# A rank for each kind of operation in attention's build-time order, and each head pair's gate projected in the pair's first two steps

## The chip, the core and the metric

The kernel runs on one core of a Trainium2 chip. The metric is the time on the device of one execution, in microseconds (us); lower is better. Seven streams of instructions matter here. PE is TensorE (matrix products and transposes; PEld is its weight load), DVE is VectorE, ACT is ScalarE, POOL is GpSimd, and SP issues the DMAs. Each engine runs its own queue strictly in order, and an instruction that waits for another engine holds up all that stands behind it in its queue.

## What is computed

A decoder trunk of two layers over 1024 tokens of width 1024: a Mamba-2 layer, then a stick-breaking attention layer, each with a residual add and a gated per-layer embedding (PLE) behind it. The change lies in the attention layer alone:

```python
def stick_breaking_mixer(h, k, v, norm_g, w_in, q_g, w_out):
    qg = rmsnorm(h, norm_g) @ w_in
    gate = qg[..., SB_WIDTH:]
    q = rmsnorm(qg[..., :SB_WIDTH].reshape(bsz, s, SB_HEADS, SB_HEAD_DIM), q_g)
    ...
    for blk in range(s // SB_BLOCK):
        z = jnp.einsum('bhtd,bhsd->bhts', q[:, :, q0:kend], k[:, :, :kend])
        ...
        log_keep = jnp.where(strict, jax.nn.log_sigmoid(-z), 0.0)
        suffix = lax.cumsum(log_keep, axis=3, reverse=True) - log_keep
        weights = jnp.where(strict, jnp.exp(jax.nn.log_sigmoid(z) + suffix), 0.0)
        outs.append(jnp.einsum('bhts,bhsd->bhtd', weights, v[:, :, :kend]))
    return (o * jax.nn.silu(gate)) @ w_out
```

There are 16 heads of 64, so 8 pairs of heads. Queries, keys, values and gate are projected from the normalized residual stream; the products are made in three terms (high times high, high times low, low times high half of each operand) for accuracy.

## The kernel before

**Stages.** The trace has the Mamba layer and its PLE first, then attention from about 926 us, then the second PLE with the rest of the output projection (`layer_b2`) from about 1646 us to the end.

**Attention's work.** The loop runs over 8 head pairs `hp`, and in each over four steps `p` = 3, 2, 1, 0, a step being two blocks of 128 tokens. Tokens are reversed, so step 3 sees the fewest keys and step 0 the most. The index `i` counts the 32 steps. One step consists of these operations, each of them one entry of a plan:

- `project` (L905): per block 24 products of 384 columns into a PSUM tile `mm` (keys, values, queries), cut into chunks of two. `copy_kq` and `copy_v` (L944, L946) take it out on ACT.
- `gate` (L905, 512 columns, 24 products a half): the pair's gate, in two halves. `sig` (L971, ACT) and `gmul` (L973, DVE) turn a half into `GT`.
- `norm`: `square` (L1010, ACT), `sums` (L1016), `start` (L1022 to L1024), three Newton turns `newton` (L1028 to L1030) and `nmul` (L1037), all on DVE.
- `values`: SP shifts V by one row (`vs`, L982 to L987), POOL subtracts and splits it (L991 to L1001).
- `flip` (L1048, PE): transposes the step's keys and queries; `k_hi` and `q_hi` (L1058, L1070, ACT) and `k_lo` and `q_lo` (L1061, L1075, DVE) split them.
- `scores` (L1104, L1105, PE): products `z` of 128 to 512 columns; `s_sig` (L1112, ACT) makes sigmoids `pt`; `scan` (L1117, DVE) runs the stick-breaking product along the row. Steps 1 and 0 have two parts a block (320 and 384, 448 and 512 columns), steps 3 and 2 one (128 and 256, 384 and 512).
- `combine`: `turn` (L1142, L1144, PE) transposes weights into `tr`; `a_hi` (L1150, ACT) and `a_lo` (L1155, DVE) split them into `wh` and `wl`; `prod` (L1163, PE) multiplies with V into `oq`; `o_copy` (L1178), `o_add` (L1183) and `o_gate` (L1190) finish the rows.
- `weights`: the next pair's weights, four loads `raw` of 512 KB (L1219), split by `w_hi` (L1238, ACT) and `w_lo` (L1242, DVE) in 16 pieces each. The `raw` tiles come from a ring of three.
- At the end `s_out` loads and splits the output weights (L1256, L1266, L1273) and `fill` multiplies two token blocks with them (48 products each, L1314; its sums are added by L1326). Behind the plan stand the PLE weights (loads L674, split L174 and L178), which take the same `raw` ring.

**What sets the order.** `Plan.order` works at build time. Of all operations whose predecessors are placed and whose ring slots are free it takes the one that could start first by its own estimates of durations; among those that could start at the same time the lowest `rank` goes first, then the one that was written first. The outcome is the order in which PE, ACT and DVE get their instructions. Ranks are 10·i plus a small number by kind: `combine` 10·i, `norm` 10·i+1, `flip` 10·i+2, `scores` 10·i+3, `project` and `gate` 10·i+5. All projections and gates are chained one behind the other in the order in which they are written (`mm_last`); in `before` the gate's two halves stand between the two blocks of step 1.

Of the kernel before, what the change touches and what calls it, by code (L numbers as in the profile page):

```python
# [18 lines left out]
P = 128  # L19
# [23 lines left out]


# [19 lines left out]
class Plan:  # L64
# [789 lines left out]
def attention(k, A, rawp, hT, oTd, dbg, b2, pairs):  # L854


    tc, nc = k.tc, k.nc
# [3 lines left out]
    with ExitStack() as ctx:  # L861
# [22 lines left out]
        op_, slot = plan.op, plan.slot  # L884
# [11 lines left out]
        def chunks(rank, us, m, make, prs, after_of, first=()):  # L896

            rec, ids = slot("mm"), []
            for c in range(0, len(prs), m):
                def go(c=c):  # L900
                    if c == 0:
                        make()
                    for i in range(c, min(c + m, len(prs))):
                        a, b, out = prs[i]()
                        nc.tensor.matmul(out, lhsT=a, rhs=b, start=(i == 0), stop=(i == len(prs) - 1))  # L905
                after = list(after_of(c, min(c + m, len(prs)) - 1))
                after += ids[-1:] if c else list(first) + mm_last[-1:]
# [9 lines left out]
        def project(i, hp, b):  # L917
            p = b // 2
            key = ("ps", hp, b)

            def make():
                tiles[key] = mm.tile([P, 512], F32, name="mm")
            sl = slice(b % 4 * P, b % 4 * P + P)
            prs = []
            for kk in range(KT):
                for t in range(3):
                    def pr(kk=kk, t=t):
                        w = sts[hp]["W"][kk]
# [3 lines left out]
            rec, ids = chunks(10 * i + 5, 0.175, 2, make, prs, wdeps(hp))  # L932
# [12 lines left out]
            a = op_("ACT", 0.37, 10 * i + 1, copy_kq, ids[-1:], takes)  # L945
            v = op_("ACT", 0.27, 10 * i + 1, lambda: nc.scalar.copy(sts[hp]["vr"][p][:, b % 2], tiles[key][:, 128:256]),  # L946
                    [a], (), (rec,))
            return a, v

        def gate(i, hp, half):  # L950
# [12 lines left out]
            rec, ids = chunks(10 * i + 5, 0.232, 2, make, prs, wdeps(hp))  # L963
# [8 lines left out]
            a = op_("ACT", 0.6, 10 * i + 2, sig, ids[-1:])  # L972
            gmul[hp, half] = op_("DVE", 0.69, 10 * i + 2, lambda: nc.vector.tensor_tensor(  # L973
                sts[hp]["GT"][:, sl], tiles[key], sts[hp]["GT"][:, sl], op=ALU.mult), [a], (), (rec,))

        def values(i, hp, p, copies):
# [12 lines left out]
            vd[i] = op_("SPV", 3.0, 10 * i, load, list(copies) + ([fgate[i - 4]] if i >= 4 else []), (vs_s,),  # L989
                        (vr_s[i - 1],) if p < 3 else ())  # L990
            sub = op_("POOL", 0.74, 10 * i, lambda: nc.gpsimd.tensor_tensor(  # L991
# [10 lines left out]
            vready[hp, p] = op_("POOL", 1.8, 10 * i, split, [sub], (V_s[i],), (vs_s,))  # L1002

        def norm(i, hp, p, copies):
# [6 lines left out]
            sq = op_("ACT", 0.63, 10 * i + 1, square, copies, (sg_s,))  # L1011
# [5 lines left out]
            rd = op_("DVE", 0.68, 10 * i + 1, sums, [sq], (), (sg_s,))  # L1017
# [20 lines left out]
            nmul[i] = op_("DVE", 0.69, 10 * i + 1, mul, [x])  # L1038

        def flip(i, hp, p):  # L1040
# [11 lines left out]
            fk = op_("PE", 0.22, 10 * i + 2, turn_(0), [nmul[i]], (ks,))  # L1052
            fq = op_("PE", 0.22, 10 * i + 2, turn_(1), [fk], (qs,), (kq_s[i],))
# [23 lines left out]
            for h in range(2):  # L1077
                prev = [op_("ACT", 0.47, 10 * i + 2, key_hi(h), [fk] + prev + (old if p == 3 else []))]
                khi[i, h] = prev[0]
                pd = [op_("DVE", 0.49, 10 * i + 2, key_lo(h), [khi[i, h]] + pd, (), (ks,))]  # L1080
                klo[i, h] = pd[0]
            for h in range(2):
                prev = [op_("ACT", 0.73, 10 * i + 2, query_hi(h), [fq] + prev, (qh_s,) if h == 0 else ())]
                pd = [op_("DVE", 0.43, 10 * i + 2, query_lo(h), prev + pd + old, (), (qs,))]
                qlo[i, h] = pd[0]
# [6 lines left out]
        def scores(i, hp, h, b, qh_s):  # L1092
# [4 lines left out]
            last = []  # L1097
            for m, (ko, w) in enumerate(parts(b)):
# [7 lines left out]
                z = op_("PE", 2 * (0.013 + w * 0.000419), 10 * i + 3, mul, [klo[i, h], qlo[i, h]] + last[:1], (z_s,), (qh_s,))  # L1106
# [6 lines left out]
                s = op_("ACT", 0.19 + w * 0.00078, 10 * i + 3, sig, [z], (pt_s[i, h, b],) if m == 0 else (), (z_s,))  # L1113
# [5 lines left out]
                last = [z, op_("DVE", 0.15 + w * 0.00208, 10 * i + 3, scan, [s] + last[1:])]  # L1119
            scans[i, h, b] = last[1]  # L1120

        def combine(i, hp, p):
            lo = 2 * p
            of_s = slot("of")
            for h in range(2):
                pr = None
                for j0 in range(lo, NT, 2):
# [17 lines left out]
                    T = op_("PE", 0.109 * c / P, 10 * i, turn_, [scans[i, h, lo], scans[i, h, lo + 1]], (tr_s,),  # L1145
# [5 lines left out]
                    H = op_("ACT", 0.2 + c * 0.00076, 10 * i, high, [T], (w_s,))  # L1151
# [4 lines left out]
                    L = op_("DVE", 0.16 + c * 0.00103, 10 * i, low, [H], (), (tr_s,))  # L1156
# [16 lines left out]
                    pr = op_("PE", 2 * c * 0.00047, 10 * i, mul, after, (), gives)  # L1173
# [5 lines left out]
                c_ = op_("ACT", 0.37, 10 * i, copy, [pr], (of_s,) if h == 0 else ())  # L1179
# [4 lines left out]
                fadd[i, h] = op_("DVE", 0.42, 10 * i, add, [c_])  # L1184
# [7 lines left out]
            fgate[i] = op_("DVE", 0.8, 10 * i, gates, [fadd[i, 0], fadd[i, 1], gmul[hp, p // 2], vd[i]], (), (of_s,))  # L1192
            if hp == 7:
                x = [fgate[i], begun[0]]
                for b in (2 * p + 1, 2 * p):
                    sl = slice(b * P, (b + 1) * P)
                    a = op_("ACT", 0.31, 10 * i, lambda b=b, sl=sl: nc.scalar.copy(b2.rows(b)[0], sts[7]["GT"][:, sl]), x)
                    rows_done[b] = op_("DVE", 0.28, 10 * i, lambda b=b, sl=sl: nc.vector.tensor_tensor(
                        b2.rows(b)[1], sts[7]["GT"][:, sl], b2.rows(b)[0].bitcast(F32), op=ALU.subtract), [a])
            elif p == 0:  # L1200
                def store():
                    nc.sync.dma_start(oTd[hp * P:(hp + 1) * P, :], sts[hp]["GT"])
                    if "oT" in dbg:
                        nc.sync.dma_start(dbg["oT"][hp * P:(hp + 1) * P, :], sts[hp]["GT"])
                stored.append(op_("SPS", 3.0, 10 * i, store, [fgate[i]]))
# [4 lines left out]
        def weights(hp, q):  # L1210

            rank = 40 * hp - 12 + 2 * q
# [7 lines left out]
            ld = op_("SPW", 3.5, rank, load, [proj[hp - 1, 7 - 2 * q][0]], (r_s,))  # L1220
            small = (4 * hp + q) % 6 == 3
            pool, bufs, seq = (pairs.more, 2, ring2) if small else (pairs.pool, 10, ring10)
            for j in range(2):
# [4 lines left out]
                for m in range(2):  # L1228
# [14 lines left out]
                    dep = [op_("ACT", 0.5, rank, high, [ld] + old + dep)]  # L1243
                    done.append(op_("DVE", 0.5, rank, low, dep, (), (r_s,)))
                wready[hp, kk] = done

        def s_out(kk):
# [9 lines left out]
            ld = op_("SPW", 3.5, rank, load, [proj[7, 5][0]], (r_s,))  # L1257
# [10 lines left out]
            a = op_("ACT", 1.06, rank, high, [ld] + old + list(first)[:1])  # L1268
# [5 lines left out]
            sdone[kk] = (a, op_(eng, us, rank, low, [a], (), (r_s,)))  # L1274
# [3 lines left out]
        def fill(t, rank, extra, takes, places):  # L1278
# [9 lines left out]
            ld = op_("SPW", 4.0, rank - 20, load, extra + stored, (r_s,) + takes)  # L1288
# [11 lines left out]
            a = op_("ACT", 1.3, rank - 20, split(0), [ld])  # L1300
            l = op_("POOL", 2.4, rank - 20, split(1), [a], (), (r_s,))
            recs = [slot("mm"), slot("mm")]
            ids = []
            for q in range(2):
                for m in range(2):
                    for c in range(0, 12, 6):
# [13 lines left out]
                        ids.append(op_("PE", 1.38, rank, go, after, takes_))  # L1320
            mm_last.append(ids[-1])
            for m in range(2):
# [5 lines left out]
                op_("DVE", 0.69, rank, add, [ids[-1]], (), (recs[m],))  # L1328
            return ids[-1]

        for hp in range(8):
            pair = [(4 * hp + 3 - p, p) for p in (3, 2, 1, 0)]
            for i, p in pair:
                copies = project(i, hp, 2 * p + 1)
                if p == 1:
                    gate(i, hp, 1)
                    gate(i, hp, 0)
# [6 lines left out]
            if hp == 6:  # L1344
                begun.append(op_("SPW", 0.0, 0, lambda: b2.begin(pairs), proj[6, 0][-1:]))
# [255 lines left out]
```

## Time and profile before

| | us |
|---|---|
| median of 3 runs (1839.4 to 1842.2) | 1841.28 |
| the profiled execution | 1838.35 |
| its span in the trace | 1836.6 |
| attention, start to the last product of `fill` | 926 to about 1646 |
| one head pair in the middle of it | about 83.5 |
| PE busy, share of the span | 95% |
| DVE busy, share of the span | 65% |

The shares are means over the whole span. In attention DVE's load is higher than its mean, and PE's lower. A time in the trace counts from the start of the span.

### The profile page before, as it was taken

The numbers are of one execution on the slowest core, as the hardware profiler recorded it, in microseconds if no ns is written. First come the engines' busy times: TensorE is split into PE (matmuls) and PEld (weight loads), VectorE is DVE, ScalarE is ACT, GpSimd is POOL, SyncE is SP. The second block draws the span as 40 slices with busy tenths as digits, with TensorE's granted clock in tenths as the row PEclk, the third lists the DMA queues.
The fourth block names the chain that finished last, engine by engine and source line by source line (L and its number), as shares of the span: only waits on it lengthen the run. The fifth ranks groups of instructions, "written<-read, shape, count | busy, mean of one in ns | idle before, by whom it ended". The sixth has DMA issues, their size and how long they took to land.

```text
span 1836.6 us, 25614 instructions
## 1 busy us (share of the span) xinstructions
PE 1740.1 (95%) x9170; PEld 1465.8 (80%) x9170; DVE 1198.9 (65%) x2460; ACT 904.5 (49%) x1976; POOL 416.6 (23%) x452
## 2 busy tenths in 40 slices
PE   7999999999999999999998989898989989789999
PEld 6777877877876877888887879898888878678887
DVE  6687278279169554345567787879787877782332
ACT  6567358349337332124456465656555555561221
POOL 0234534524625122200011110111111012220110
PEclk9999999999999999999999999999999999899999
DMA  4223213223212754322211111111111112151110
GB/s 155 66 81 92 81 62 94 92 60 96 92 52 87 245 158 149 116 97 76 95 41 29 53 29 41 31 43 30 53 43 31 44 38 64 61 175 62 50 38 35
DMA packets 96399, 139.43 MB, mean 76 GB/s; under 512 B 18160, under 2 KB 66640, under 8 KB 96272
## 3 DMA queue, kind: packets, MB, share of 16 engines
q1 hardware_dynamic: 96272, 137.80, 23.4%
q8 instruction: 72, 1.18, 0.3%
q14 instruction: 55, 0.45, 0.1%
HBM read 108.77 MB, written 24.77 MB: 73 GB/s over the span
## 4 chain that ended last, share of the span: by engine, by line
PE 78%; DVE 14%; ACT 5%; issue 2%; DMA 2%; POOL 0%; SPq 0%; DVEq 0%; ACTq 0%
PE mm L48 37%; PE mm L905 18%; PE mm L1432 4%; DVE pt L1117 3%; PE oq L1163 3%; PE pq L48 2%; PE z L1105 2%; DVE v L304 2%; PE intra L479 2%; DVE wl L1155 2%; PE z L1104 2%; PE tr L1142 1%; PE inter L474 1%; PE tr L734 1%; PE tr L1144 1%
## 5 line engine op out<-in xcount | busy, mean ns | idle before, releaser
L48 PE MATMUL mm<-ul,wh 128*128 128x512 f32 (+1 forms) x648 | 254.0, 392 | 0.0
L48 PE MATMUL mm<-uh,wl 128*128 128x512 f32 (+1 forms) x648 | 252.4, 390 | 0.0
L48 PE MATMUL mm<-uh,wh 128*128 128x512 f32 (+1 forms) x648 | 252.4, 389 | 0.1
L1117 DVE TENSOR_TENSOR_SCAN pt<-pt,keep 128x320 f32<-128x320 f32 (+3 forms) x192 | 190.8, 1021 | 7.9 <-ACT pt L1112 2.5
L905 PE MATMUL mm<-g0h,hh 128*128 128x384 f32 x512 | 177.1, 346 | 0.0
L905 PE MATMUL mm<-g0l,hh 128*128 128x384 f32 x512 | 176.1, 344 | 0.7 <-DVE g0l L1242 0.7
L905 PE MATMUL mm<-g0h,hl 128*128 128x384 f32 x512 | 176.2, 344 | 0.0
L304 DVE SCALAR_TENSOR_TENSOR v<-u,convh,v 128x512 f32<-128x512 f32 x144 | 129.5, 904 | 55.1 <-ACT v L302 52.6
L991 POOL TENSOR_TENSOR vs<-vs,vr 128x256 f32<-128x256 f32 x32 | 23.9, 747 | 559.7 <-DMA vs<-vr 182.7
L48 PEld LDWEIGHTS mm<-ul,wh 128*128 128x128 f32 x648 | 121.7, 188 | 26.1 <-issue 2.3
L48 PEld LDWEIGHTS mm<-uh,wh 128*128 128x128 f32 x648 | 121.7, 188 | 25.7 <-issue 1.1
L48 PEld LDWEIGHTS mm<-uh,wl 128*128 128x128 f32 x648 | 121.8, 188 | 25.6 <-issue 1.9
L176 POOL TENSOR_TENSOR wl<-raw,wh 128x1024 fp32r<-128x1024 f32 x39 | 95.3, 2443 | 156.0 <-ACT wh L174 156.0
L1150 ACT CAST wh<-tr 128x512 fp32r<-128x512 f32 (+1 forms) x160 | 82.5, 548 | 71.3 <-PE tr L1144 71.1
L1155 DVE TENSOR_TENSOR wl<-tr,wh 128x512 fp32r<-128x512 f32 (+1 forms) x160 | 96.6, 632 | 22.9 <-ACT wh L1150 21.7
L1112 ACT ACTIVATE pt<-z 128x320 f32<-128x320 f32 (+3 forms) x192 | 88.7, 490 | 45.8 <-PE z L1105 45.2
L644 DVE SCALAR_TENSOR_TENSOR acc<-mm,rg,acc 128x512 f32<-128x512 f32 x64 | 47.9, 749 | 84.5 <-PE mm L48 83.4
L905 PEld LDWEIGHTS mm<-g0l,hh 128*128 128x128 f32 x512 | 98.0, 191 | 1.8 <-DVE g0l L1242 1.1
L905 PEld LDWEIGHTS mm<-g0h,hh 128*128 128x128 f32 x512 | 98.1, 192 | 1.1
L905 PEld LDWEIGHTS mm<-g0h,hl 128*128 128x128 f32 x512 | 97.7, 191 | 0.5
L717 DVE SCALAR_TENSOR_TENSOR pth<-pth,pq 128x512 f32<-128x512 f32 (+1 forms) x33 | 22.2, 672 | 114.5 <-PE pq L48 109.7
L1104 PE MATMUL z<-kst,qh 128*128 128x320 f32 (+3 forms) x192 | 75.4, 394 | 13.4 <-ACT qh L1070 5.7
(378 smaller groups left out, 4347.6 us busy)
## 6 DMA issues: line engine op xcount, KB each, us to landing
raw<-in_w_in SPq DMA_DIRECT2D x40, 512.0 KB
ex<-acd SPq DMA_DIRECT2D x64, 256.0 KB
raw<-in_w_b SPq DMA_DIRECT2D x32, 512.0 KB
raw<-in_m_out SPq DMA_DIRECT2D x16, 512.0 KB
raw<-in_gate SPq DMA_DIRECT2D x16, 512.0 KB
graw<-gT SPq DMA_DIRECT2D x30, 256.0 KB
gT<-zs SPq DMA_DIRECT2D x28, 256.0 KB
acc<-in_x SPq DMA_DIRECT2D x8, 512.0 KB
```

Of the source, the lines that this page charges most:

```text
L48: nc.tensor.matmul(out, lhsT=a, rhs=b, start=(i == 0), stop=(i == n - 1))
L176: (eng or nc.gpsimd).tensor_tensor(lo, raw, hi.bitcast(F32), op=ALU.subtract)
L304: nc.vector.scalar_tensor_tensor(vv, u[:, 3 - j:3 - j + 512], w(j), vv, op0=ALU.mult, op1=ALU.add)
L644: nc.vector.scalar_tensor_tensor(acc[:, sl], ps, k.rg[:, g, t:t + 1], acc[:, sl], op0=ALU.mult, op1=ALU.add)
L905: nc.tensor.matmul(out, lhsT=a, rhs=b, start=(i == 0), stop=(i == len(prs) - 1))
L1104: nc.tensor.matmul(z[:, :w], lhsT=tiles["qh", i][:, h, qs], rhs=rk, start=True, stop=False)
L1112: nc.scalar.activation(tiles[key][:, ko:ko + w], tiles["z", i, h, b, m][:, :w], AF.Sigmoid, scale=-1.0)
L1117: nc.vector.tensor_tensor_scan(pt[:, ko:ko + w], pt[:, ko:ko + w], keep[:, ko:ko + w], pt[:, ko - 1:ko] if ko else 1.0, op0=ALU.mult, op1= ...
L1150: nc.scalar.copy(wh[:, :c], tiles["tq", key][:, :c])
L1155: nc.vector.tensor_tensor(wl[:, :c], tiles["tq", key][:, :c], wh[:, :c].bitcast(F32), op=ALU.subtract)
L1163: nc.tensor.matmul(out[:, :w], lhsT=sts[hp]["V"][j // 2][:, j % 2, h * P:(h + 1) * P], rhs=rhs, start=(j0 == lo and m == 0), stop=(j0 == N ...
L1432: nc.tensor.matmul(pss[n], lhsT=a, rhs=b, start=(q == 0 and i == 0), stop=(q == 1 and i == 11))
```

## The change

It adds a table `RANK` with a number for each kind of operation, names the kind in each call of `op`, and adds the number to the rank. The numbers are large for some kinds (`k_hi` -2745, `s_sig` -2535, `gmul` -1807), so that these always go first among operations that could start at once; `project` gets -12, `turn` +12, `prod` -51, `scores` and `gate` nothing. It moves the two halves of the gate from step 1 to steps 3 and 2, and makes the second sigmoid of a block wait for the first.

```diff
+RANK = {"project": -12, "copy_kq": -19, "copy_v": 14, "square": -25, "sums": -1396, "start": -2,
+        "newton": -1683, "v_sub": -24, "sig": 30, "gmul": -1807, "w_load": -67, "w_hi": -23, "w_lo": -9,
...
-    def op(self, eng, us, rank, fn, after=(), takes=(), gives=()):
-        self.ops.append((eng, us, rank, fn, tuple(after), tuple(takes), tuple(gives)))
+    def op(self, kind, eng, us, rank, fn, after=(), takes=(), gives=()):
+        self.ops.append((eng, us, rank + RANK.get(kind, 0), fn, tuple(after), tuple(takes), tuple(gives)))
...
-            fk = op_("PE", 0.22, 10 * i + 2, turn_(0), [nmul[i]], (ks,))
+            fk = op_("flip", "PE", 0.22, 10 * i + 2, turn_(0), [nmul[i]], (ks,))
...
-                s = op_("ACT", 0.19 + w * 0.00078, 10 * i + 3, sig, [z], (pt_s[i, h, b],) if m == 0 else (), (z_s,))
+                s = op_("s_sig", "ACT", 0.19 + w * 0.00078, 10 * i + 3, sig, [z] + sg, (pt_s[i, h, b],) if m == 0 else (), (z_s,))
...
                 copies = project(i, hp, 2 * p + 1)
-                if p == 1:
+                if p == 3:
                     gate(i, hp, 1)
+                if p == 2:
                     gate(i, hp, 0)
```

The number of instructions on each engine stays the same. Three places show what moves. Lines of the changed kernel are 6 to 8 higher than those of `before`.

**First, PE in a middle pair, where step 1 ends and step 0 begins.** `oq` rows are `prod`, `tr<-ident,kq` is `flip`, `tr<-ident,pt` is `turn`, `z` rows are `scores`, `mm` rows are projections (of 384 columns) or gates (of 512) with `hh` and `hl`, the two halves of the normalized stream, and `g0h` and `g0l`, those of the weights. Before:

```order
L1163 MATMUL oq<-wh,V 128x256 x2
L1163 MATMUL oq<-wl,V 128x256 x2
L1048 MATMUL tr<-ident,kq 128x128 x4
L1104 MATMUL z<-kst,qh 128x448
L1105 MATMUL z<-kst,ql 128x448
L1104 MATMUL z<-kst,qh 128x448
L1105 MATMUL z<-kst,ql 128x448
L905 MATMUL mm<-g0h,hh_6971 128x384
L905 MATMUL mm<-g0l,hh_6971 128x384
L1104 MATMUL z<-kst,qh 128x512
```

In the changed kernel, where step 1's first head is turned and multiplied:

```order
L1152 MATMUL tr<-ident,pt 128x128
L911 MATMUL mm<-hh_6970,g0l 128x512
L911 MATMUL mm<-hh_6970,g0h 128x512
L911 MATMUL mm<-hl_6972,g0h 128x512
L911 MATMUL mm<-hh_6970,g0l 128x512
L911 MATMUL mm<-hh_6970,g0h 128x512
L911 MATMUL mm<-hl_6972,g0h 128x512
L1111 MATMUL z<-kst,qh 128x448
L1112 MATMUL z<-kst,ql 128x448
L1171 MATMUL oq<-wh,V 128x256
```

Before, the flip and the scores that come of it stand next to each other, right behind the last products of step 1. Now six products of a gate and step 0's scores stand between step 1's turns and their products. From the fifth pair on, 14 projection products and eight of `prod` stand between the last flip of a step 0 and its first scores.

**Second, DVE near the end of attention.** `hl<-raw,hh` is the low half of an `s_out` load (the last of the two that DVE makes), `pt` rows are scans, `g0l<-raw,plen,g0h` is the low half of a PLE weight. Before:

```order
L1273 TENSOR_TENSOR hl_15597<-raw,hh_15596 128x1024
L1117 SCALAR_TENSOR_TENSOR pt<-pt,keep 128x448 x2
L1117 SCALAR_TENSOR_TENSOR pt<-pt,keep 128x512 x2
L1117 SCALAR_TENSOR_TENSOR pt<-pt,keep 128x448 x2
L178 SCALAR_TENSOR_TENSOR g0l<-raw,plen,g0h 128x512 x2
```

In the changed kernel:

```order
L1281 TENSOR_TENSOR hl_15513<-raw,hh_15512 128x1024
L184 SCALAR_TENSOR_TENSOR g0l<-raw,plen,g0h 128x512 x2
L1191 TENSOR_TENSOR of<-oq,of 64x256
L1163 TENSOR_TENSOR wl<-tr,wh 128x384
L1163 TENSOR_TENSOR wl<-tr,wh 128x512 x2
L1198 SCALAR_TENSOR_TENSOR GT<-of,v_15109,GT 128x128 x2
L1124 SCALAR_TENSOR_TENSOR pt<-pt,keep 128x448
```

Six scans stood between the two kinds; now the first PLE weight stands right behind the `s_out` half.

**Third, PE at the start of attention**, after the first block's 24 products. Before:

```order
L905 MATMUL mm<-g0h,hh_6971 128x384
L905 MATMUL mm<-g0l,hh_6971 128x384
L905 MATMUL mm<-g0h,hl_6973 128x384
L905 MATMUL mm<-g0h,hh_6971 128x384
L905 MATMUL mm<-g0l,hh_6971 128x384
```

In the changed kernel:

```order
L911 MATMUL mm<-g0h,hh_6971 128x384
L911 MATMUL mm<-g0l,hh_6971 128x384
L911 MATMUL mm<-g0h,hl_6973 128x384
L911 MATMUL mm<-hh_6971,g0h 128x512
L911 MATMUL mm<-hl_6973,g0h 128x512
```

The gate's first half now follows the first block, where the step's second block followed before.

## Rows read from the trace of the kernel before

**Rows 1.** The page's part 1: busy us, share of the span, instructions.
```profile
PE 1740.1 (95%) x9170; PEld 1465.8 (80%) x9170; DVE 1198.9 (65%) x2460; ACT 904.5 (49%) x1976; POOL 416.6 (23%) x452
```

**Rows 2.** Busy time by stretch: stretch, length, PE, PEld, DVE, ACT, POOL, PE clock.
```profile
926.00:1031.90 105.90, 96.58 (x557) 86.80 (x556) 80.51 (x190) 57.66 (x137) 10.40 (x20) 0.97 0.14 41
...
1114.50:1198.50 84.00, 78.00 (x457) 71.39 (x457) 68.84 (x151) 48.01 (x115) 10.37 (x21) 0.96 0.13 38
...
1448.90:1532.70 83.80, 77.54 (x457) 71.14 (x456) 67.40 (x149) 44.89 (x107) 10.16 (x20) 0.96 0.12 39
```

**Rows 3.** The same view, its last line over the six middle periods, 1031.9 to 1532.7.
```profile
sum 500.80, PE 466.09 PEld 426.45 DVE 408.58 ACT 285.41 POOL 65.48; mean PE 77.68 PEld 71.08 DVE 68.10 ACT 47.57 POOL 10.91
```

**Rows 4.** PE's timeline, 1161 to 1175: start, us, instruction, [idle before <-releaser].
```profile
1162.70 0.45 PE L1163 MATMUL oq<-wl,V 128*128 128x256 f32 x2 [0.72 <-DVE wl L1155]
...
1167.55 0.44 PE L1163 MATMUL oq<-wl,V 128*128 128x256 f32 x2 [0.44 <-DVE wl L1155]
...
1171.17 0.63 PE L1048 MATMUL tr<-ident,kq 128*128 128x128 f32 x4 [1.93 <-DVE kq L1037]
1173.49 0.71 PE L1104 MATMUL z<-kst,qh 128*128 128x448 f32 x1 [1.69 <-DVE kst L1061]
1174.60 0.74 PE L1105 MATMUL z<-kst,ql 128*128 128x448 f32 x1 [0.41 <-DVE ql L1075]
```

**Rows 5.** Busy time by stretches of 4 us there, columns as in Rows 2.
```profile
1164.00:1168.00 4.00, 2.87 (x20) 2.10 (x19) 3.83 (x11) 2.71 (x6) 0.00 (x0) 1.00 0.08 24
1168.00:1172.00 4.00, 1.87 (x12) 1.32 (x11) 3.73 (x12) 0.75 (x2) 2.19 (x5) 1.00 0.02 8
1172.00:1176.00 4.00, 2.11 (x5) 1.55 (x6) 3.62 (x9) 2.56 (x7) 0.28 (x1) 0.65 0.00 0
1176.00:1180.00 4.00, 4.00 (x13) 3.57 (x12) 3.79 (x5) 1.98 (x4) 0.00 (x0) 0.50 0.45 131
```

**Rows 6.** The chain of waits in order of time: start, us, what.
```profile
1127.73 2.80 PE mm L905 x12
...
1142.40 9.36 PE mm L905 x54
...
1639.50 5.53 DMA raw<-in_proj
```

**Rows 7.** Busy time in attention's end by stretch, columns as in Rows 2.
```profile
1576.00:1600.00 24.00, 16.22 (x86) 13.83 (x84) 19.92 (x34) 13.66 (x28) 9.76 (x12) 0.85 0.15 49
1600.00:1612.00 12.00, 9.16 (x25) 5.69 (x25) 11.52 (x16) 8.70 (x21) 4.27 (x3) 0.58 0.27 85
...
sum 112.50, PE 93.04 PEld 78.30 DVE 91.74 ACT 63.10 POOL 32.44; mean PE 15.51 PEld 13.05 DVE 15.29 ACT 10.52 POOL 5.41
```

**Rows 8.** Timelines of DVE, SP and ACT in the same end.
```profile
1605.28 1.22 DVE L1273 TENSOR_TENSOR hl<-raw,hh 128x1024 fp32r<-128x1024 f32 x1
1606.42 8.34 DVE L1117 TENSOR_TENSOR_SCAN pt<-pt,keep 128x448 f32<-128x448 f32 x6
...
1606.58 13.49 SPq L674 DMA_DIRECT2D raw<-in_gate  x4
...
1614.98 0.72 ACT L174 ACTIVATE g0h<-raw,plen 128x512 fp32r<-128x512 f32 x1 [1.36 <-DMA raw<-in_gate]
```

**Rows 9.** Timelines of DVE and POOL: one kind of step beside POOL's work and apart from it.
```profile
1150.28 0.69 DVE L1037 TENSOR_TENSOR kq<-kq,kry 128x512 f32<-128x512 f32 x1
...
1169.80 1.22 DVE L1037 TENSOR_TENSOR kq<-kq,kry 128x512 f32<-128x512 f32 x1
...
1169.75 0.72 POOL L991 TENSOR_TENSOR vs<-vs,vr 128x256 f32<-128x256 f32 x1 [11.71 <-ACT of L1178]
```

**Rows 10.** Timelines of SP and POOL: a load of shifted values and its first use.
```profile
1584.34 0.64 SPq L982 DMA_DIRECT2D vs<-vr  x1
...
1592.60 0.78 POOL L991 TENSOR_TENSOR vs<-vs,vr 128x256 f32<-128x256 f32 x1 [5.83 <-DMA vs<-vr]
```

**Rows 11.** Groups of DVE's instructions in one pair, 1114.5 to 1198.5: count, busy us, mean ns.
```profile
L1242 DVE SCALAR_TENSOR_TENSOR g0l<-raw,sn,g0h 128x256 fp32r<-128x256 f32 x8 | 3.9, 488 | 0.1
```

More of the change, by code (lines that the diff above doesn't have):

```diff
@@ L42 @@
 CHUNKS = {29: (0, 1), 30: (2, 3)}
+RANK = {"project": -12, "copy_kq": -19, "copy_v": 14, "square": -25, "sums": -1396, "start": -2,
+        "newton": -1683, "v_sub": -24, "sig": 30, "gmul": -1807, "w_load": -67, "w_hi": -23, "w_lo": -9,
+        "flip": -671, "k_hi": -2745, "k_lo": 7, "q_hi": -732, "q_lo": -1398, "s_sig": -2535, "scan": 17,
+        "turn": 12, "a_hi": 54, "a_lo": 11, "prod": -51, "o_copy": -1, "o_add": -15, "o_gate": 40, "store": 8,
+        "r_hi": 20, "r_lo": -4, "o_hi": 14, "o_lo": 4, "f_split": 12, "fill": -9, "f_add": -20}
 def split3(nc, out, pairs):
@@ L971, in sig @@
                 nc.scalar.activation(st["GT"][:, sl], tiles[key], AF.Sigmoid)
-            a = op_("ACT", 0.6, 10 * i + 2, sig, ids[-1:])
-            gmul[hp, half] = op_("DVE", 0.69, 10 * i + 2, lambda: nc.vector.tensor_tensor(
+            a = op_("sig", "ACT", 0.6, 10 * i + 2, sig, ids[-1:])
+            gmul[hp, half] = op_("gmul", "DVE", 0.69, 10 * i + 2, lambda: nc.vector.tensor_tensor(
                 sts[hp]["GT"][:, sl], tiles[key], sts[hp]["GT"][:, sl], op=ALU.mult), [a], (), (rec,))
@@ L1001, in split @@
                     nc.gpsimd.tensor_tensor(Vx[:, j, 1:3], d[:, j], Vx[:, j, 0::3].bitcast(F32), op=ALU.subtract)
-            vready[hp, p] = op_("POOL", 1.8, 10 * i, split, [sub], (V_s[i],), (vs_s,))
+            vready[hp, p] = op_("v_split", "POOL", 1.8, 10 * i, split, [sub], (V_s[i],), (vs_s,))
         def norm(i, hp, p, copies):
@@ L1030, in turn_ @@
                 nc.vector.scalar_tensor_tensor(y, s, 1.5, y, op0=ALU.add, op1=ALU.mult)
-            x = op_("DVE", 0.6, 10 * i + 1, start, [rd])
+            x = op_("start", "DVE", 0.6, 10 * i + 1, start, [rd])
             for _ in range(3):
-                x = op_("DVE", 0.6, 10 * i + 1, turn_, [x])
+                x = op_("newton", "DVE", 0.6, 10 * i + 1, turn_, [x])
             def mul():
@@ L1037, in mul @@
                 nc.vector.tensor_tensor(kq, kq, g["y"].unsqueeze(2).broadcast_to([P, m, 64]), op=ALU.mult)
-            nmul[i] = op_("DVE", 0.69, 10 * i + 1, mul, [x])
+            nmul[i] = op_("nmul", "DVE", 0.69, 10 * i + 1, mul, [x])
         def flip(i, hp, p):
@@ L1118, in scan @@
                                                  pt[:, ko - 1:ko] if ko else 1.0, op0=ALU.mult, op1=ALU.max)
-                last = [z, op_("DVE", 0.15 + w * 0.00208, 10 * i + 3, scan, [s] + last[1:])]
+                sg = [s]
+                last = [z, op_("scan", "DVE", 0.15 + w * 0.00208, 10 * i + 3, scan, [s] + last[1:])]
             scans[i, h, b] = last[1]
@@ L1150, in high @@
                         nc.scalar.copy(wh[:, :c], tiles["tq", key][:, :c])
-                    H = op_("ACT", 0.2 + c * 0.00076, 10 * i, high, [T], (w_s,))
+                    H = op_("a_hi", "ACT", 0.2 + c * 0.00076, 10 * i, high, [T], (w_s,))
                     def low(key=key, c=c):
@@ L1172, in combine @@
                         gives += [V_s[i - q] for q in range(4)]
-                    pr = op_("PE", 2 * c * 0.00047, 10 * i, mul, after, (), gives)
+                    pr = op_("prod", "PE", 2 * c * 0.00047, 10 * i, mul, after, (), gives)
                 def copy(h=h):
@@ L1242, in low @@
                         nc.vector.scalar_tensor_tensor(lo[:, sl], part(), g, hi[:, sl].bitcast(F32), op0=ALU.mult, op1=ALU.subtract)
-                    dep = [op_("ACT", 0.5, rank, high, [ld] + old + dep)]
-                    done.append(op_("DVE", 0.5, rank, low, dep, (), (r_s,)))
+                    dep = [op_("w_hi", "ACT", 0.5, rank, high, [ld] + old + dep)]
+                    done.append(op_("w_lo", "DVE", 0.5, rank, low, dep, (), (r_s,)))
                 wready[hp, kk] = done
@@ L1267, in s_out @@
             first = sdone.get(kk - 1, ())
-            a = op_("ACT", 1.06, rank, high, [ld] + old + list(first)[:1])
+            a = op_("o_hi", "ACT", 1.06, rank, high, [ld] + old + list(first)[:1])
             eng, us = ("DVE", 1.25) if kk in (5, 7) else ("POOL", 2.4)
@@ L1287, in load @@
                 g["parts"], g["o"] = places(), {}
-            ld = op_("SPW", 4.0, rank - 20, load, extra + stored, (r_s,) + takes)
+            ld = op_("f_load", "SPW", 4.0, rank - 20, load, extra + stored, (r_s,) + takes)
             def split(hi_lo):
@@ L1299, in split @@
                 return go
-            a = op_("ACT", 1.3, rank - 20, split(0), [ld])
-            l = op_("POOL", 2.4, rank - 20, split(1), [a], (), (r_s,))
+            a = op_("f_split", "ACT", 1.3, rank - 20, split(0), [ld])
+            l = op_("f_split", "POOL", 2.4, rank - 20, split(1), [a], (), (r_s,))
             recs = [slot("mm"), slot("mm")]
@@ L1319, in fill @@
                         takes_ = tuple(recs) if not ids else ()
-                        ids.append(op_("PE", 1.38, rank, go, after, takes_))
+                        ids.append(op_("fill", "PE", 1.38, rank, go, after, takes_))
             mm_last.append(ids[-1])
@@ L1344, in attention @@
             if hp == 6:
-                begun.append(op_("SPW", 0.0, 0, lambda: b2.begin(pairs), proj[6, 0][-1:]))
+                begun.append(op_("begin", "SPW", 0.0, 0, lambda: b2.begin(pairs), proj[6, 0][-1:]))
             for i, p in pair:
```

59 lines of the change are left out of this document (30 added, 29 removed).

## The prediction

> **What bounds the kernel now.** I read the page's first part, then attention in stretches, then PE's own timeline at the place where it idles, and last the chain. PE is busy for 95% of the span, DVE for 65% [rows 1], so PE is the bound, and an order can give back only what PE idles or runs slowly. In attention PE idles more: 6.0 us in a middle pair of 84.0, 6.3 in a later one, 9.3 in the first stretch of 105.9 [rows 2]. Over six middle periods PE is busy for 77.68 us of 83.47, DVE for 68.10 and ACT for 47.57 [rows 3]: 5.8 us idle, eight pairs in a row.
>
> PE's timeline says where. It waits for `wl` (0.72 and 0.44), for `nmul`'s keys (1.93), for `kst` (1.69) and for `ql` (0.41) [rows 4], all within 13 us, and all for DVE. That is one chain: the products of step 1, whose operands DVE splits, then the flip of step 0, then the split of what was flipped, then step 0's scores, which stand directly behind the flip. DVE is busy for 3.83, 3.73 and 3.62 of each 4 us there, while PE is busy for 2.87, 1.87 and 2.11 [rows 5]: for 12 us the two work in turn, and DVE sets the pace. Behind it comes a second cost. PE's granted clock is 1.00 until 1172, then 0.65, then 0.50, the lower of the levels of 2.4 and 1.2 GHz [rows 5]; it fell after the stretches in which PE had been busy half the time. Of 2.11 us at 0.65 and 4.00 at 0.50, 0.35 x 2.11 + 0.5 x 4.00 = 2.7 us are lost. Without waits and at full clock a pair would need 77.7 - 2.7 = 75.0 us.
>
> **The change, part by part.** No instruction is added or removed, so each term is a wait or a slow stretch.
>
> *Step 1 to step 0.* Before, the scores of step 0 stand right behind its flip, and four rows of `prod` right ahead of it. In the changed order 14 projection products and eight of `prod` stand between the flip and those scores: 14 x 0.173 (54 took 9.36 us [rows 6]) = 2.4 us, and some 1 us for the products of `prod` (two took 0.45 [rows 4], the later half of them narrower). That covers the 1.69 + 0.41 us for `kst` and `ql`. Six gate products and step 0's first scores stand between step 1's turns and its products: 6 x 0.233 (12 took 2.80 [rows 6]) = 1.4 us, above the 0.72 and 0.44 for `wl`. What is late next is DVE's own queue: PE now needs some 75 us a pair and DVE 68, so DVE has 7 us of slack in the sum, but both run in order, and every read of one by the other must fit. The keys' 1.93 us hang on that: `nmul` ends the Newton chain on DVE, and if DVE's rows stand too early or too late, this wait moves to another flip. I leave 1.5 us of waits in a pair, between none and the 5.8 of before, nearer to none because the long waits have 3.4 us of cover. With idle stretches that short I expect the clock to stay at 1.00. A pair is then 75.0 + 1.5 = 76.5 us, or 7.0 less. Six middle pairs and the first one, whose stretch idles as much [rows 2], give 7 x 7.0 = **49 us**. The last pair is the tail's.
>
> *The tail.* From 1532.7 to 1645.2 PE is busy for 93.04 of 112.5 us, so it idles 19.5; in its middle the clock is 0.85 and 0.58, which takes 0.15 x 16.22 + 0.42 x 9.16 = 6.3 us more [rows 7]. Before, 54 `fill` products stood behind the last `prod`; in the changed order 18 do, and 36 stand among the last scores, where PE idled: 36 x 0.233 = 8.4 us [rows 6] leave the end. Against it stands the first PLE weight's low half on DVE, now directly behind the last low half of `s_out` instead of behind six scans. That half frees the `raw` tile which the PLE load needs: the half ended at 1605.28 + 1.22, the load was issued at 1606.58 [rows 8]. So DVE will stand there until a load has landed (5.53 us for one such [rows 6]) and ACT has made the high half (0.72 [rows 8]), 6.2 us at most, with scans and splits queued behind it, for which the last turns on PE wait. On ACT the high half stands ahead of scores' sigmoids in the same way. The sum is 8.4 + 6.3 - 6.2 = 8.5 if the clock comes back. The ends are -5 (no clock, and the stall whole, with 1 us more for the shorter cover of the last flips) and +20 (all idle time). I take **+9**.
>
> *The start.* The gate's first half goes ahead of the second block of step 3, so the first scores come 24 x 0.233 = 5.6 us later. PE has products all the while; what is lost is only what DVE and ACT cannot catch up. Between 0 and -5.6, I take **-2**, since PE's own idle time, not DVE's, sets the first pair's length [rows 2]. The second sigmoid's wait for the first costs nothing: ACT runs them in that order anyway.
>
> *Loads.* A load of shifted values takes from 1584.34 to 1592.60, 8.3 us, to its first use [rows 10], with a whole step of cover. Unmoved in the sum.
>
> The sum is 49 + 9 - 2 = 56 us, against the profiled execution of 1838.35: 1782. The median of the runs is 2.9 us (0.16%) above that execution, so against the median it is 1841.3 - 56 = **1785 us**. The terms' own ends (a pair between 74.9 and 78.5, the tail's as above) give 1768 to 1806.
>
> **The rivals.**
>
> *Full cover.* All of PE's waits go, and with them the half clock: 75.0 us a pair, 7 x 8.5 = 59.5, and 20 in the tail, -2 at the start: 1841.3 - 77.5 = **1764**. For it: each wait in [rows 4] is shorter than the work now standing in front of it. Against it: DVE's queue is as rigid as PE's, and any row of it that stands too far ahead costs PE a wait.
>
> *DVE and POOL get in each other's way.* One `nmul` takes 0.69 us apart from POOL's work, and 1.22 beside POOL's subtraction, which had begun 0.05 us earlier and lasted 0.72 [rows 9]. So far such overlaps cost little, since DVE idles 15.4 us a pair. In the changed order DVE has hardly any idle time for POOL's 10.91 us a pair [rows 3] to fall into; if all of it blocks DVE, DVE needs 68.1 + 10.9 = 79.0 us and becomes the bound: 7 x 4.5 = 31.5, 5 in the tail (DVE has most work there too), -2: 1841.3 - 34.5 = **1807**. Against it: the longer `nmul` is within the 68.1 already, so a part of the 10.9 is counted twice. The Trainium skill, "SBUF — State Buffer", section "SBUF: two separate sides", has it that a DVE operation with two SBUF inputs and a GpSimd operation that reads SBUF exclude each other for a whole instruction. By that rule the `nmul` of [rows 9] should have waited out POOL's remaining 0.67 us; the trace shows 0.53, so it nearly agrees.
>
> *The weights come late (slower).* The place is ACT, where a fourth high half `w_hi` waits in order for its load, which on SP stands behind the shifted values' load. If that wait were whole, it would be 8.3 [rows 10] + 5.53 [rows 6] = 13.8 us a pair, 7 x 13.8 = 97 in all, and the time 1841.3 - 56 + 97 = **1882**. It outweighs the gain from 56 / 7 = 8 us a pair on. Against it: the load needs the `raw` tile that the first quarter's low halves free, and at least 24 rows of DVE stand between these and the next quarter's; at 0.488 each, the length of such a low half [rows 11], that is 11.7 us, against 5.53 for the load. No such wait is in the trace of before.
>
> *No effect.* The waits only move to other flips, and the pair stays at 83.5: **1841**. The order speaks against it, since DVE's 68.1 would leave 15 us a pair idle as before.
>
> **How the numbers follow.** The forecast gets 0.61, full cover 0.17, DVE and POOL 0.11, late weights 0.07, no effect 0.04. The predicted time is the forecast's. The range leaves out the last two, the upper fringe of the third and the lower fringe of the second: 1754 to 1813. A measurement of this kernel can tell about 0.2% (3.7 us) from no change. The first three cases are faster, so faster has 0.89, the same 0.04, slower 0.07.
>
> **What would show it.** In a middle pair of the changed kernel PE should be busy for about 75 us of 76.5 with a granted clock of 1.00 throughout, and no wait of over 0.5 us at a flip or at step 0's scores. If the period is right but the clock still falls, the split between waits and clock was wrong. DVE should stand 4 to 6 us ahead of its first PLE low half, near the last `s_out` half; if it doesn't, the tail's term is too small. A longer mean of DVE's two-input rows at unchanged counts would show the second rival, an ACT wait for a `raw` load in every pair the third. The prediction is wrong at its root if PE's waits are short and yet the pair stays above 80 us, for then the products themselves, not the waits, hold PE.

## The result, and the profile after

The changed kernel takes 1760.09 us (1757.63 to 1760.66) against 1840.99 for the kernel before: a ratio of 0.9558 with a 95% interval of 0.9542 to 0.9575, 81 us less. The forecast was 1785, with 1754 to 1813 around it. Its sign, its place (attention's pairs) and its range held; its gain of 56 us is two thirds of the real one. The time is nearest to the rival that I called full cover (1764).

The page's part 1 and the clock's row of part 2, kernel after, answer [rows 1]:

```profile
PE 1699.9 (97%) x9170; PEld 1449.6 (83%) x9170; DVE 1193.8 (68%) x2460; ACT 896.1 (51%) x1976; POOL 422.5 (24%) x452
...
PEclk9999999999999999999999999999999999899999
```

PE has the same 9170 products and is busy for 40 us less (1740.1 before), while the span is 80.7 us shorter. So half of the gain is time in which PE idled, and half is time in which it counted as busy and wasn't needed.

To see where, I cut attention at the first flip of each pair. The kernel before has these flips at 942.26, 1031.35, ..., 1532.07; the tail behind the last of them is cut at 1645.30, three products ahead of the end of `fill` (1645.85). Kernel before, by stretch (stretch, length, PE, PEld, DVE, ACT, POOL, PE clock, DMA):

```profile
1031.35:1532.07 500.72, 466.01 (x2731) 426.38 (x2730) 408.44 (x893) 285.33 (x677) 64.85 (x120) 0.96 0.12 37
1532.07:1645.30 113.23, 93.77 (x476) 79.00 (x475) 92.44 (x168) 63.41 (x136) 33.07 (x32) 0.91 0.33 106
```

The same view of the kernel after, whose flips stand at 947.53, 1017.41, ..., 1453.12 and whose `fill` ends at 1565.86. The row of four periods and the tail's answer [rows 3] and [rows 7]:

```profile
947.53:1017.41 69.88, 68.98 (x421) 64.36 (x420) 58.71 (x132) 45.78 (x112) 11.44 (x20) 1.00 0.11 32
...
1156.72:1453.12 296.40, 293.10 (x1837) 277.73 (x1835) 272.23 (x601) 184.29 (x449) 50.60 (x84) 1.00 0.15 45
...
1453.12:1564.90 111.78, 93.53 (x521) 82.40 (x520) 99.96 (x169) 63.65 (x141) 30.27 (x27) 0.91 0.26 84
```

The last four whole pairs take 296.40 / 4 = 74.1 us each, PE busy for 73.3 of them, at a clock of 1.00; before, a pair took 83.45, PE busy for 77.7, at 0.96. Seven pairs, flip to flip, shrink from 589.8 to 505.6 us, by 84.2; the first flip comes 5.3 us later, and the tail, taken to the end of `fill`, is 1.0 us shorter (113.8 and 112.7). These three make up 80 of the 80.7.

The stretches don't hold the same work in both kernels, though. Ahead of the first flip PE is busy for 21.0 us instead of 15.8, with 0.5 us idle in either kernel: the 5.3 us of delay are work. The tail holds 34 more turns (they start 0.11 us apart), 44 more products of `prod` (0.12) and 4 more of the projections (0.173 [rows 6]), but 38 fewer gate products (0.233 [rows 6]): about 1 us more work. So the pairs are lighter by some 6 us, and at equal work the tail gains about 2 us and a pair (84.2 - 6) / 7 = 11 us, rather than 12.

PE's timeline where the kernel before had its 12 us of turn and turn about [rows 4], in a late pair of the kernel after (start, us, instruction, [idle before <-releaser]):

```profile
1287.52 0.34 PE L1112 MATMUL z<-kst,ql 128*128 128x384 f32 x1
1287.70 0.34 PE L911 MATMUL mm<-g0h,hl 128*128 128x384 f32 x1
1287.88 0.34 PE L911 MATMUL mm<-g0h,hh 128*128 128x384 f32 x1
1288.05 0.38 PE L1054 MATMUL tr<-ident,kq 128*128 128x128 f32 x2
1288.19 0.42 PE L1171 MATMUL oq<-wh,V 128*128 128x256 f32 x2
...
1291.65 0.37 PE L1111 MATMUL z<-kst,qh 128*128 128x448 f32 x1
```

The last flip of step 0 starts at 1288.05, its first scores at 1291.65, 3.6 us later, and no row between them shows an idle time. Of PE's 27.8 us of waits from 1030 to 1450 in the kernel before, 3.4 are left (listed by who waits, for whom: us, times, longest; before, then after):

```profile
PE tr L1048 <- DVE kq L1037: 8.9, 5, 1.9
PE oq L1163 <- DVE wl L1155: 5.8, 10, 0.8
PE z L1104 <- ACT qh L1070: 4.1, 3, 1.4
PE z L1104 <- DVE kst L1061: 3.4, 2, 1.7
PE tr L1142 <- DVE pt L1117: 2.3, 5, 0.5
PE z L1105 <- DVE ql L1075: 2.2, 5, 0.5
PE tr L1142 <- DVE krv L1022: 1.1, 5, 0.2
```

```profile
PE tr L1054 <- DVE wl L1163: 2.0, 3, 0.8
PE z L1111 <- DVE kst L1067: 0.9, 1, 0.9
PE z L1112 <- DVE ql L1081: 0.5, 1, 0.5
```

In three of the five pairs of this stretch, step 0's first scores waited for ACT's high half of the queries (`qh`), not for DVE as in the pair of [rows 4].

### The profile page after: what moved, and what is told of

Read it like the earlier page. It is cut to its first block, busy times and chain, and to the rows that moved or that the text cites. A ratio compares the mean times of both kernels' runs of the same rounds, so it can differ in the third digit from the quotient of the medians.

```text
span 1755.9 us, 25570 instructions
## 1 busy us (share of the span) xinstructions
PE 1699.9 (97%) x9170; PEld 1449.6 (83%) x9170; DVE 1193.8 (68%) x2460; ACT 896.1 (51%) x1976; POOL 422.5 (24%) x452
## 4 chain that ended last, share of the span: by engine, by line
PE 81%; DVE 10%; DMA 3%; ACT 3%; issue 2%; POOL 0%; SPq 0%; DVEq 0%; ACTq 0%; POOLq 0%
PE mm L54 38%; PE mm L911 18%; PE mm L1441 4%; PE oq L1171 4%; PE pq L54 3%; PE intra L485 2%; DVE v L310 2%; PE tr L1150 2%; PE z L1112 2%; PE z L1111 2%; DVE pt L1124 1%; PE tr L1152 1%; PE inter L480 1%; PE tr L740 1%; DMA raw<-in_gate 1%
## 5 line engine op out<-in xcount | busy, mean ns | idle before, releaser
L997 POOL TENSOR_TENSOR vs<-vs,vr 128x256 f32<-128x256 f32 x32 | 29.4, 918 | 468.1 <-DMA vs<-vr 228.7
L447 ACT ACTIVATE ex<-ex,acum 128x128 f32<-128x128 f32 x256 | 86.5, 389 | 0.8
```

Of the source, the lines that this page charges most:

```text
L447: nc.scalar.activation(x, x, AF.Relu, bias=acum[:, c:c + 1])
```

## The experiments

**Which part of the change does it.** Four kernels: the table without the gate's move, the move without the table, and the table's two halves (both with the move).

```diff
 # rank_only: RANK as in the change
-                if p == 3:
+                if p == 1:
                     gate(i, hp, 1)
-                if p == 2:
                     gate(i, hp, 0)
 # gate_only
+RANK = {}
 # big_ranks: the entries beyond 600; small_ranks: the others
+RANK = {'sums': -1396, 'newton': -1683, 'gmul': -1807, 'flip': -671, 'k_hi': -2745, 'q_hi': -732, 'q_lo': -1398, 's_sig': -2535}
```

> The table of ranks (and the second sigmoid's wait) without the gate's move: both halves of the gate stay between the blocks of step 1. Theory A: what the change gives comes from other products of PE between the last flip of step 0 and its first scores; by the products that the order shows there (1.9 to 3.7 us in the middle pairs, 0.2 before, 3.3 to 4.5 in the changed kernel) nearly all of the wait of 2.1 us for the split is covered, so at least 50 of the 81 us stay: 1770 to 1790. Theory B: the gate's place decides (its 48 long products are now where step 2 and 3 need cover, and the step-1 blocks stand closer together), the ranks only rearrange: 1820 or more.

> The gate's move and the second sigmoid's wait with an empty table of ranks. Cover between flip and scores of step 0 by the order: 1.3 us. Theory A: 1.1 us of wait goes per pair and some of the slow clock behind it, some 2 us a pair: 1820 to 1830. Theory B: 1790 or less.

> The changed kernel with only the eight ranks beyond 600 (sums, newton, gmul, flip, k_hi, q_hi, q_lo, s_sig): the chain from the norm to the scores goes first on DVE and ACT, PE's own order is left to the estimates. Cover by the order: 0.6 us. Theory A (cover on PE): little above the gate's move alone, 1815 to 1835. Rival C (the wait is DVE's: 1.93 us for the norm's end and 1.69 for the split go as soon as DVE serves that chain first): 1780 to 1800.

> The changed kernel with only the other ranks (project -12, turn +12, prod -51 and the like). Cover by the order: 4.2 us at step 0, 5.4 at step 1. Theory A: the split's wait is covered whole, 1765 to 1785. Rival C: the norm chain on DVE still comes as late as before, the flip's wait of 1.9 us stays, 1805 to 1825.

| kernel | us | ratio to before, 95% interval | PE's waits, 1030 to 1450, us |
|---|---|---|---|
| rank_only | 1761.5 | 0.9565 [0.9551, 0.9579] | 2.7 |
| gate_only | 1856.7 | 1.0084 [1.0069, 1.0099] | 34.6 |
| big_ranks | 1855.8 | 1.0074 [1.0057, 1.0091] | 32.7 |
| small_ranks | 1779.3 | 0.9662 [0.9647, 0.9676] | 8.1 |

The table gives 79 us by itself, more than theory A had for it (1770 to 1790). The gate's move by itself costs 16 us, and beside the table it is worth nothing that these runs can tell (1760.1 and 1761.5). Theory B, that the gate's place decides, has fallen, and so has my expectation that the move alone would win a little (1820 to 1830): its 48 long products a pair no longer stand in step 1, and the waits behind it grow. The largest waits of gate_only, PE, 1030 to 1450:

```profile
PE tr L1050 <- DVE kq L1039: 14.9, 5, 3.0
PE oq L1167 <- DVE wl L1159: 10.5, 9, 1.7
PE mm L907 <- DVE g0l L1246: 5.1, 5, 1.5
```

The wait of step 0's flip for `nmul` grew from 1.8 to 3.0 us a pair, and a wait of the next pair's projections for their weights came in (5.1 us in five pairs, none before): the rival of late weights in small, on DVE's low halves.

The eight large ranks with the move do nothing measurable beyond the move (1855.8 and 1856.7), where theory A had 1815 to 1835. They do serve the norm's chain first: PE's waits for `nmul` fall from 14.9 to 0.7 us. But those for `wl` rise from 10.5 to 16.6 and those for scans from 1.5 to 6.1, and the sum hardly changes. Rival C, that serving this chain first on DVE is what counts, falls by that. On top of the small ranks they still give 19 us (1779.3 to 1760.1).

**Is it the early weights?** Theory D has it that in the kernel before nothing stood between step 0's flip and its scores because the pair's own projections were used up there and the next pair's wait for weights. Three of the small ranks bring these weights forward.

```diff
 # weights_only, the gate as before
+RANK = {'w_load': -67, 'w_hi': -23, 'w_lo': -9}
 # no_weights: the whole table but these three, the gate as before
```

> Only the three ranks of the next pair's weights (w_load -67, w_hi -23, w_lo -9), everything else zero, the gate in its old place. Theory D, formed after the first four runs: before, PE has nothing to put between step 0's flip and its scores because the pair's own projections are used up and the next pair's wait for their weights; earlier splits of the weights let them in. The order shows 2.8 us of products between that flip and its scores instead of none, so the wait for the split goes, and with it the slow clock: 1775 to 1800. Rival E (the many ranks that make step 1's combine yield on ACT and DVE do it, the weights only help): 1815 to 1835.

> All ranks but those three, the gate in its old place. The order still shows 2.2 to 2.6 us of products between the flip and the scores of step 0 in the middle pairs. Theory D in its strict form (without early weights nothing is to be had): 1815 or more. Theory A (the products between flip and scores decide, wherever they come from): 1765 to 1790.

weights_only: 1815.2, ratio 0.9864 [0.9850, 0.9879], in the range of rival E. no_weights: 1765.4, ratio 0.9600 [0.9586, 0.9614]. Theory D falls in its strict form: without early weights 74 us stay. But theory A doesn't fit whole either, since weights_only has 2.8 us of products behind step 0's flip and wins 25 us only, with a clock of still 0.96 in the four pairs from 1191 to 1519. PE's largest waits in weights_only, 1030 to 1450, say why:

```profile
PE tr L1146 <- DVE pt L1120: 12.1, 10, 1.5
PE oq L1167 <- DVE of L1187: 2.9, 5, 0.6
PE z L1108 <- DVE ql L1077: 2.7, 6, 0.8
```

The waits at the flip and for `kst` are gone, and in their place PE waits for scans at the turns (2.3 us in the kernel before). The waits of weights_only come to 24.7 us in all, those of no_weights to 3.3. So it takes other ranks than those of the weights to cover the steps' three meetings of PE and DVE (flip to scores, scan to turn, low half to product). Which of them are needed for that was not run one by one.

**What the slow clock costs.** The kernel before, with fillers on PE where it waits at step 0: transposes of a constant that nobody reads, 16 ahead of the flip and 16 or 20 behind it.

```diff
 # warm and warm2, flip: turn_(0) of step 0
+                    if p == 0 and m == 0:
+                        for _ in range(16):
+                            nc.tensor.transpose(full[:, 256:384], ident, ident)
 # warm: 16 more in turn_(1), behind the queries' flip; warm2: in scores, ahead of the products
+                    if b == 1 and h == 0 and m == 0:
+                        for _ in range(20):
+                            nc.tensor.transpose(z[:, :P], ident, ident)
```

> The kernel before with 32 more PE transposes of a constant in each pair: 16 ahead of step 0's flip and 16 behind it, 1.7 us each, where PE waits 1.93 and 2.1 us. Nobody reads them. If the slow clock behind these waits is a cost of its own, as the prediction had it, the granted clock of a middle pair goes from 0.96 to 1.00 and the time falls by 2.7 us a pair, 19 to 23 us: 1818 to 1825. If the clock doesn't follow from these waits, or the chain through DVE absorbs it, the time stays at 1841 or rises by what the fillers overshoot, up to 1850.

> The kernel before with fillers that delay nobody: 16 transposes of a constant ahead of step 0's flip as in the last run, and 20 (2.2 us) ahead of step 0's first scores, written into those scores' own tile, so that ACT's split of the queries doesn't wait for them (in the last run it did, by some 0.8 us). If the slow clock is a cost of its own: granted clock 1.00 in the middle pairs and 1818 to 1825. Theory G, after the last run: in that stretch DVE's queue sets the pace (busy 3.6 to 3.9 of each 4 us), PE's slow products run under DVE's rows, and a faster PE only waits longer for DVE: 1835 to 1843 at a clock of 1.00.

warm: 1842.1, ratio 1.0011 [1.0001, 1.0021]; inconclusive, since its second fillers kept ACT from the queries' split (the first scores waited 0.83 us for `qh`), and in some pairs the clock still fell. warm2: 1831.4, ratio 0.9952 [0.9937, 0.9966], 9 us less, between the two ranges. warm2, first a middle pair, then the two 4-us stretches that stood at 0.65 and 0.50 in [rows 5]:

```profile
1195.59:1277.37 81.78, 79.36 (x493) 73.19 (x492) 68.47 (x151) 47.75 (x114) 10.50 (x21) 1.00 0.13 40
...
1172.00:1176.00 4.00, 3.57 (x26) 2.99 (x24) 3.21 (x8) 2.90 (x8) 1.09 (x3) 1.00 0.00 0
1176.00:1180.00 4.00, 4.00 (x22) 3.62 (x21) 3.79 (x5) 2.73 (x8) 0.00 (x0) 1.00 0.42 133
```

A pair takes 81.8 instead of 83.45 us: the clock costs 1.7 us of time a pair. The first pair is 0.9 us longer (89.95 against 89.09), so it is 9 in all. In busy time, the 36 fillers take 3.8 us (they start at 1169.39 and 1171.57, and what follows them at 1171.13 and 1173.67), which leaves 79.4 - 3.8 = 75.6 against 77.7: 2.1 us, where I had worked out 2.7 from two stretches. Theory G falls in its strict form: DVE, as busy there as before, takes back at most the 0.4 us between 2.1 and 1.7. It may be less, since the fillers' 3.8 us stand where PE's idle time fell by only 3.4 (5.8 to 2.4).

**What bounds the changed kernel.** The same kernel with 3.1 us more of PE a pair, or 3.4 us more of DVE, once far from PE's next need (low halves of weights made twice) and once between flip and scores (low halves of queries made twice).

```diff
 # more_pe, turn_(0) of every step
+                        for _ in range(7):
+                            nc.tensor.transpose(full[:, 256:384], ident, ident)
 # more_dve_off, the low half of a weight
+                        for _ in range(1 + (kk < 7 and sl.start == 0)):
 # more_dve_on, the low half of the queries
+                    for _ in range(2):
```

> The changed kernel with 28 more transposes of a constant on PE in each pair, seven ahead of each step's flip: 28 x 0.11 = 3.1 us a pair, 24 us in all eight. If PE is the bound of the changed kernel's pairs: 20 to 26 us longer, 1780 to 1787. If DVE's queue is what is full: under 12 us.

> The changed kernel with seven of a pair's sixteen low halves of weights made twice: 7 x 0.49 = 3.4 us more of DVE a pair, 24 us in seven pairs, on work that PE needs much later. DVE goes from 68.2 to 71.6 of some 73.5 us. If DVE's queue has the slack that the busy times show: under 8 us longer, 1760 to 1768. If DVE sets the pace whatever is in its queue: 20 to 26 us longer.

> The changed kernel with the low half of the queries made twice: 8 x 0.42 = 3.4 us more of DVE a pair, 27 us in all, between the flip and its scores. If the products between flip and scores still cover it: as much as the last one, 1760 to 1770. If the chain itself is tight: 1775 to 1790, with PE waiting for ql.

more_pe: 1780.95, 20.9 us more of 24 added. more_dve_off: 1773.9, 13.8 more of 24. more_dve_on: 1775.9, 15.8 more of 27. PE is the bound, nearly us for us. But DVE's slack of 6 us a pair by busy times (68.1 of 74.1) is worth far less than it looks: more than half of each added us comes through, wherever in the chain it stands. The first of my expectations for DVE missed low (1760 to 1768); the time of the second lies at the near end of its tight case (1775 to 1790), but not by the wait that I named, since PE waits for `ql` for 0.9 us from 1030 to 1450, against 0.5. Here, with two queues run in order, a busy share of 92% had slack for less than half of what was added.

**The tail.** There DVE is busy for 99.96 of 111.78 us, and some of its rows are long. I cut POOL's long subtractions of the end into pieces of 256 columns.

```diff
 # pool_pieces, s_out's low half on POOL (and f_split in the same way)
-                (nc.vector if eng == "DVE" else nc.gpsimd).tensor_tensor(lo[:, sl], v(), hi[:, sl].bitcast(F32), op=ALU.subtract)
+                    for x in range(2):
+                        for c in (slice(0, 256), slice(256, 512)):
+                            nc.gpsimd.tensor_tensor(lo[:, 2 * j + x, c], v()[:, x, c], hi[:, 2 * j + x, c].bitcast(F32), op=ALU.subtract)
```

> The changed kernel with POOL's long subtractions of the end (the low halves of the output weights, 2.4 us each, and of the two last blocks' rows) cut into pieces of 256 columns, about 0.6 us each, with the same work in all. In the trace of the changed kernel a DVE row that meets such a subtraction lasts as long as it: two rows of 0.3 us take 2.73 us together beside one of 2.83, a row of 0.15 us takes 2.23 beside one of 2.37, and so on, some 9 us in the end, where DVE is busy almost throughout. Theory H: a DVE row waits for the instruction of POOL that it meets, so with short ones it waits 0.6 us at most and others slip in between: no DVE row lengthened by over 0.8 us, 1753 to 1758. Rival: DVE waits as often as there are pieces, or the end is not DVE's: 1759 to 1763.

1758.1 (1757.6 to 1762.6), ratio 0.9565 [0.9551, 0.9578]: not to be told from the changed kernel. No DVE row is lengthened by over 0.8 us any more, as theory H had it, and DVE's busy time in the tail fell by 3.4 us. But the tail stayed at 111.9:

```profile
sum 111.88, PE 93.29 PEld 81.65 DVE 96.61 ACT 64.20 POOL 35.63; mean PE 13.33 PEld 11.66 DVE 13.80 ACT 9.17 POOL 5.09
```

So the end is not DVE's alone. The chain of waits in the changed kernel alternates (start, us, what):

```profile
1501.88 8.64 DMA vs<-vr
1510.67 1.29 POOL vs L997
...
1513.38 2.35 POOL hl L1281
1515.74 3.32 DMA raw<-oTd
...
1528.32 1.33 DVE g0l L184 x2
1529.67 4.65 DMA raw<-in_gate
1534.34 1.34 ACT g0h L180 x2
```

## Why the prediction was right, and where it was short

**The place and the mechanism held.** PE's waits at step 0 are gone, the clock of the middle pairs is 1.00, and both come from other products put between PE's and DVE's meetings: in the six partial kernels the time is the shorter the fewer of PE's waits are left. What did not hold is theory A's narrow form, that the flip's own scores are the one place that counts (weights_only).

**The term that failed is the pair: 7.0 us forecast, about 11 measured at equal work**, so 49 against 78 us in the seven. Of the two numbers in it, the 1.5 us of waits left was near: 296.40 - 293.10 = 3.3 us in four pairs, 0.8 each. The floor of 75.0 was wrong: PE is busy for 73.3 us, and with 459 products a pair against 455. I had taken PE's busy time, less the slow clock, for work. warm2 measures that very number, 75.6, at full clock and with 2.4 us of waits still there; the other 2.3 us go when the waits go. more_dve_on shows the same the other way round. Its last four pairs hold as many products as those of the changed kernel (1837), at the same clock:

```profile
1163.42:1468.58 305.16, 297.72 (x1837) 277.86 (x1835) 285.32 (x632) 184.44 (x449) 53.87 (x85) 1.00 0.14 44
```

They are 8.8 us longer; 4.1 of these are idle time of PE, and 4.6 count as its busy time. A row that shows how this can come about is `z<-kst,ql` at 448 columns: 0.47 us behind a wait in warm2, 0.37 in a run of such products, which start 0.20 apart. A product alone counts with its whole passage, and in a run only with its distance to the next. That this makes up all of the 2.3 us is argued, not measured. So each wait cost more than its idle time, and full cover would have been worth more than I gave it. The first pair, which I had taken for one like the others, was 89.1 us long and gave more than they did.

**The tail's term of 9 failed too, the other way: about 2 us came.** PE idles 18.3 us of the tail instead of 19.5, and the clock did not come back: 0.91 before and after. Nor did the one loss in the term, the stall of up to 6.2 us on DVE: the first load was issued before the `s_out` half ended, into another tile, and DVE went on at once (kernel after, DVE, answering [rows 8]).

```profile
1527.12 1.20 DVE L1281 TENSOR_TENSOR hl<-raw,hh 128x1024 fp32r<-128x1024 f32 x1
1528.23 1.41 DVE L184 SCALAR_TENSOR_TENSOR g0l<-raw,plen,g0h 128x512 fp32r<-128x512 f32 x2
```

The dependence itself is in the chain above, one load later and on ACT: the low half of 1528.32 frees a tile, the load takes 4.65 us, and the high half behind it holds ACT. And a wait that I had put at nothing is there: a load of shifted values stands in the chain for 8.64 us, and behind its use on POOL the low half `hl` and the next `raw` load. In the tail's chain of the kernel before no such load stands. How much of the missing 7 us these waits cost was not tested.

**The start**: the first flip is 5.3 us later, with 5.3 us more of work done by then, so next to nothing is lost; I had taken 2.

**The sum and its range.** The 56 us were 29 short in the pairs, 7 over in the tail and 2 short at the start, so a part of the pair's error was hidden by luck. The ends of the terms, added up, give 1761 to 1817, not 1768 to 1806, and the pair's own ends (74.9 and 78.5) come from no row.

**The rivals.** Full cover is nearest to what came, but by two errors that offset each other: 59.5 us in the pairs, where 78 came, and 20 in the tail, where 2 came. DVE and POOL: in the pairs POOL pays, not DVE. DVE's busy time a pair is 68.1 before and after, POOL's goes from 10.9 to 12.7; its subtraction of values (L997) takes 0.92 us on the mean, 0.75 before. Late weights showed in gate_only, at 1 us a pair.

## What to carry to other kernels

Where two engines that run in order meet several times in a loop, cover all of the meetings or the wait moves to the next one; a part of a change that costs 16 us alone can be free beside the rest. A busy time taken from a stretch with waits is not a floor: the products next to a wait count longer, and a slow clock behind it counts too. And measure slack by adding work: here DVE at 92% gave less than half of an added microsecond for nothing.

## What the runs showed of the hardware

A DVE row with operands in SBUF alone that starts while a long POOL subtraction runs is held until that ends. In the changed kernel's tail, first DVE's timeline, then POOL's:

```profile
1479.33 2.73 DVE L1198 SCALAR_TENSOR_TENSOR GT<-of,v,GT 128x128 f32<-128x128 f32 x2
...
1486.59 0.15 DVE L1028 TENSOR_SCALAR krv<-kss 128x8 f32<-128x8 f32 x1
...
1493.06 0.61 DVE L1198 SCALAR_TENSOR_TENSOR GT<-of,v,GT 128x128 f32<-128x128 f32 x2
...
1501.57 2.23 DVE L1028 TENSOR_SCALAR krv<-kss 128x8 f32<-128x8 f32 x1
```

```profile
1478.82 2.83 POOL L1281 TENSOR_TENSOR hl<-raw,hh 128x1024 fp32r<-128x1024 f32 x1
...
1501.41 2.37 POOL L1281 TENSOR_TENSOR hl<-raw,hh 128x1024 fp32r<-128x1024 f32 x1 [4.32 <-ACT hh L1274]
```

The pair of `o_gate` rows takes 0.61 us apart from POOL and 2.73 beside it; a row of eight elements takes 0.15 and 2.23. This is the exclusion that the Trainium skill states ("SBUF — State Buffer", section "SBUF: two separate sides"), for the whole instruction, and the trace agrees; the row of eight elements has one input, so the wait is not confined to rows with two (that page of the Trainium skill also names modes of DVE that use both ports; whether this row ran in one, no run here shows). Rows that read PSUM are not held: three `wl<-tr,wh` take 1.75 us together from 1472.90 on, beside a POOL subtraction of 2.35 us that starts at 1473.35. With POOL's work in pieces (pool_pieces) short rows wait for one piece after another: five rows that take 0.17 us elsewhere take 0.67 each from 1466.11 on, beside six pieces of 4.25 us together. So the pieces took 3.4 us off DVE's busy time in the tail, though the end didn't come earlier.
